# Two 32-row matrix products of a chunk inverse written as full-height products, and the instruction order seeded from a table in the source

## The chip, the cores and the metric

One NeuronCore of a Trainium2 chip runs the whole program in one launch. The time is device microseconds from launch to end, as the median of several executions of the same built program. Beside it stands one profiled execution, whose span runs from its first to its last recorded instruction. The engines have short names in the profile: PE is the matrix engine (PEld its weight loads), DVE the vector engine, ACT the scalar engine, POOL the GpSimd engine and SP the queue that issues the transfers.

## The reference, cut to what matters

The layer is a decoder mixer with two groups of heads, run over 4096 positions of width 1024: one input projection, a gated linear attention group, an RWKV-7 group, one output projection with residual, and two RMS norms. The change touches the RWKV group alone, whose reference is a recurrence over positions:

```python
def _rwkv7_scan(r, decay, k, v, kk, a):
    """S_t = S_{t-1} (diag(w_t) - kk_t^T (a_t * kk_t)) + v_t^T k_t ;  y_t = S_t r_t."""
    def step(S, inp):
        r_t, w_t, k_t, v_t, kk_t, a_t = inp
        sa = jnp.einsum('bhvk,bhk->bhv', S, -kk_t)
        S = (S * w_t[:, :, None, :]
             + sa[..., None] * (kk_t * a_t)[:, :, None, :]
             + v_t[..., None] * k_t[:, :, None, :])
        y = jnp.einsum('bhvk,bhk->bhv', S, r_t)
        return S, y
    _, y = lax.scan(step, S0, xs)
```

Within a chunk of 64 positions the terms `sa` depend on each other through a strictly triangular 64x64 matrix per head, so that a chunk needs the inverse of a unit triangular matrix. The kernel works by chunks and computes that inverse.

## The kernel before

The sequence is cut into 8 blocks of 512 positions. In a block the RWKV heads come as 4 pairs; a pair of heads in one block is a unit, 32 units in all, and a unit has 8 chunks of 64 positions. The two heads of a pair lie in rows 0 to 63 and 64 to 127 of every tile.

Several streams of work are recorded side by side: the weight splitter, the normalisation of x, the projections and preparation of a unit (`rwkv_ab`), the inverse (`rwkv_i`), the chain over the chunks (`rwkv_c`), what follows it (`rwkv_d`), the attention group and the output blocks. The projections are float16 matmuls with 512 moving columns, three for each product, because each operand is split in a high and a low half; the small products of the RWKV unit are float32. A matmul of `both` or `duo` is a pair: the same 128 rows, with weights 64 columns wide in the left and in the right half of the array, which run side by side. That is the shape 128x64 (rows by columns of weights) in the profile, and projections and chain products all have it. Other products use the array in other shapes: 64x128, 64x64, 128x32, 128x128 (transposes) and 32x32.

The inverse of a unit goes in three steps. `rwkv_ab` fills the tile `nb` (`Nb` in the profile) with the triangular matrices from products `DD,bk`, and sends their 32x32 diagonal blocks through memory (`nd`) into a tile `f`. POOL inverts these blocks by a recurrence of 31 steps with two operations each (`tm`, `Tc`), and the result goes through memory again (`td`) back into the diagonal blocks of `nb`. For the last unit alone the recurrence runs on DVE. Then `rwkv_i` makes the block off the diagonal, which is a product of three 32x32 matrices for each head and chunk:

```python
            for q0 in (0, 64):
                V.transpose(Ta[q0:q0 + 32], nb[q0:q0 + 32, :, q0:q0 + 32])
            for c in range(NC):
                for q0 in (0, 64):
                    T.matmul(pl[q0 + 32:q0 + 64, 0, c, :], lhsT=nb[q0:q0 + 32, c, q0 + 32:q0 + 64], rhs=Ta[q0:q0 + 32, c, :],
                             start=True, stop=True)
            V.tensor_copy(Vs, pl[:, 0])
```

and a second set of 16 such products from `Vs` (the same buffer as `Ta`) against `nb`, which ACT copies into `nb`. The first 16 are called the first product below, the second 16 the second product. `rwkv_c` then runs the 8 chunks of the unit one after the other, with three pairs of products per chunk (`ch<-sv,DD`, `ch<-us,Nb`, `ch<-uv,bk`), where ACT or DVE must move each result before the next pair can start.

The order on every engine is made by the program itself while it is built. Each operation is recorded with its predecessors, its engine and an assumed duration. `forward` is a list scheduler over these, with a rank for each operation and two parameters, `keep` (how much a matmul of the shape that PE is in is preferred) and `look` (how far ahead an engine looks). `backward` makes ranks from the other end. `build(guide)` records the streams again so that they follow the start times of an earlier round, which also decides which PSUM bank a stage gets. Before, 11 rounds were run, starting from no guide, and the order whose modelled end was earliest was kept; the instructions were then issued in the order of their modelled start. Every engine works its instructions strictly in that order, and waits where an input is late.

Of the kernel before, what the change touches and what calls it, by code (L numbers as in the profile page):

```python
# [3 lines left out]

# [6 lines left out]
F32 = mybir.dt.float32  # L11
# [3 lines left out]
U8 = mybir.dt.uint8  # L15
# [6 lines left out]
P = 128  # L22
# [3 lines left out]
C = 64  # L26
# [12 lines left out]
SO = 0.3  # L39
# [6 lines left out]
PB = {"ch": 1, "y": 1}  # L46
NBK = 6
NC = TB // C
LOOKS = ((1.0, 0.15),)
PASSES = 5  # L50
PUT_OFF = 1.0
ROUNDS = (LOOKS,) * 11
GUP = 2.0 ** 19
DECAY = math.exp(-0.5)

# [25 lines left out]
CK_GM = 896  # L81
CK_SEL = 1408
NCK = 1536


@with_exitstack
def hymba_kernel(ctx, tc, xT, wt, wg, wo, wua, gup, pk, ck, out):
    nc = tc.nc
    nc.scalar.preload_act_table_set("exp_and_others")
    NT = out.shape[1]  # L90
    NB = NT // TB

    one = ctx.enter_context(tc.tile_pool(name="one", bufs=1))
# [3 lines left out]
    rt = ctx.enter_context(tc.tile_pool(name="rt", bufs=1))  # L97
# [10 lines left out]
    def build(guide):  # L108
# [21 lines left out]
        def parts(ap):  # L130
            if ap.tensor.name == out.tensor.name:
                return []
            if ap.space == DRAM:
                return dram(ap)
            a = ap.start_partition()
            tag = ap.tensor.name.rsplit("_", 1)[0].rstrip("0123456789_")
            if tag in TABLES:
                w = math.prod(ap.tensor.shape[1:])
                return [(ap.tensor.name, i) for i in range(ap.offset % w, ap.offset % w + math.prod(ap.shape[1:]))]
            if tag in FINE:  # L140
                q = FINE[tag]
                return [(ap.tensor.name, h) for h in range(a // q, (a + ap.shape[0] - 1) // q + 1)]
            hs = range(a // 64, (a + ap.shape[0] - 1) // 64 + 1)
            if ap.tensor.name in HEADS:
                o = ap.offset % P // 64
                e = range(2) if ap.ap[-1][1] > 64 else range(o, o + 1)
                return [(ap.tensor.name, h, i) for h in hs for i in e]
            if ap.tensor.name in XS:
                o = ap.offset % (4 * TB) // TB
                e = range(o, o + max(1, math.prod(ap.shape[1:]) // TB)) if ap.dtype == F16 else range(4)  # L150
                return [(ap.tensor.name, h, 2 + i) for h in hs for i in e]
            return [(ap.tensor.name, h) for h in hs]
# [324 lines left out]
        def after(*what):  # L477

            t = 0.0
            for x in what:  # L480
                if isinstance(x, tuple):
                    r = ring.get((x[0], F32))
                    for i in range(x[1] if r else 0):
                        y = r[1][(r[0] + i) % len(r[1])]
                        t = max([t] + [used.get(k, 0.0) for k in parts(y)])
                else:
                    t = max([t] + [ready.get(k, (0.0, ""))[0] for k in parts(x)])
            return t + EL
# [28 lines left out]
        V, S, G, T, D = (Engine(n, e) for n, e in (("V", nc.vector), ("S", nc.scalar), ("G", nc.gpsimd), ("T", nc.tensor), ("D", nc.sync)))  # L517
        lo, hi = slice(0, 64), slice(64, 128)
# [22 lines left out]
        def sb(pool, shape, dt, tag, bufs=1):  # L541

            key = (tag, dt)
            if key not in store:
                store[key] = [pool.tile(shape, dt, tag=f"{tag}_{i}", name=f"{tag}_{i}") for i in range(bufs)]
            if key not in ring:
                ring[key] = [0, store[key]]
            r = ring[key]
            t = r[1][r[0] % len(r[1])]
            r[0] += 1  # L550
            return t
# [5 lines left out]
        f3 = lambda t: t.rearrange("p (c t) -> p c t", c=NC)  # L557
# [26 lines left out]
        for g in range(4):  # L584
            q = slice(32 * g, 32 * g + 32)
# [30 lines left out]
        Gst = [sb(one, [P, P], F32, f"Gst{j}") for j in range(2)]  # L616
        for t in Sst + Gst:
            G.memset(t, 0.0)
        NBUF = 2
        DD = [sb(un, [P, NC, 2, P], F32, f"DD{i}") for i in range(NBUF)]  # L620
        HEADS.update(t.tensor.name for t in DD)
        De, Do = ([t[:, :, :, 64 * e:64 * e + 64] for t in DD] for e in range(2))
        uv1 = sb(un, [P, NC, 2, 64], F32, "uv")
        Nb = [sb(un, [P, NC, 192], F32, f"Nb{i}") for i in range(NBUF)]
        SC = [sb(un, [P, 4, P], F32, f"SC{i}") for i in range(2)]
        for i in range(NBUF):
            G.memset(De[i], 0.0)
# [183 lines left out]
        def rel(st):  # L811
            banks.extend(held.pop(st, []))

        def need(st, n=1):

            rel(st)
            put_off = False
            while True:
                if len(banks) < n:
                    yield lambda: len(banks) >= n  # L820
                banks.sort(key=(lambda t: leave.get(t.tensor.name, 0.0)) if guide else bank_free)
                if len(banks) >= n and (guide or bank_free(banks[n - 1]) <= now[0]):
                    t = leave.get(banks[n - 1].tensor.name, 0.0)
                    if guide and not put_off and t > due(cur[0])[0] + PUT_OFF:
                        put_off = True
                        yield (t,)
                        continue
                    break
                if len(banks) >= n:
                    yield bank_free(banks[n - 1])  # L830
            held[st] = [banks.pop(0) for _ in range(n)]
            return held[st] if n > 1 else held[st][0]
# [98 lines left out]
        def rwkv_ab(u, p, b, xs, LR):  # L931
            de, do, nb = De[u % NBUF], Do[u % NBUF], Nb[u % NBUF]
            cs_ = slice(P * p, P * p + P)
# [131 lines left out]
            for k, q in enumerate((lo, hi)):  # L1065
                for e, o in enumerate((hi, lo)):
                    S.copy(sv[o, k::2, e, :], pv[q, :, e, :])
            units[u] = (DD[u % NBUF], nb, sv, bk, PC, bv, tg)
            done["A"] += 1
# [10 lines left out]

        def rwkv_i(nb):

            Ta = Vs = sb(rt, [P, NC, 32], F32, "Ta", 1)
            yield after(nb)
            for q0 in (0, 64):
                V.transpose(Ta[q0:q0 + 32], nb[q0:q0 + 32, :, q0:q0 + 32])
            yield after(Ta)
            pl = (yield from need("i")).rearrange("p (a c t) -> p a c t", a=2, c=NC)
            for c in range(NC):
                for q0 in (0, 64):  # L1090
                    T.matmul(pl[q0 + 32:q0 + 64, 0, c, :], lhsT=nb[q0:q0 + 32, c, q0 + 32:q0 + 64], rhs=Ta[q0:q0 + 32, c, :],
                             start=True, stop=True)
            V.tensor_copy(Vs, pl[:, 0])
            yield after(Vs)
            for c in range(NC):
                for q0 in (0, 64):
                    T.matmul(pl[q0:q0 + 32, 1, c, :], lhsT=Vs[q0 + 32:q0 + 64, c, :], rhs=nb[q0 + 32:q0 + 64, c, q0 + 32:q0 + 64],
                             start=True, stop=True)
            for q0 in (0, 64):
                S.copy(nb[q0:q0 + 32, :, q0 + 32:q0 + 64], pl[q0:q0 + 32, 1])  # L1100
            rel("i")
# [444 lines left out]
        def stream_i():  # L1546
            for u in range(4 * NB):
                yield lambda: u in invs_
                done["IS"] += 1
                yield from rwkv_i(invs_.pop(u))  # L1550
                done["I"] += 1
# [37 lines left out]
        return steps, forward, backward  # L1589

    with tc.manual_schedule(engines={getattr(mybir.EngineType, e) for e in ("PE", "DVE", "Activation", "Pool", "SP")}):
        guide, best = {}, None
        for looks in ROUNDS:
            steps, forward, backward = build(guide)
            first_order = forward([s.t0 for s in steps])
            mine = first_order
            for keep, look in looks:
                start, end = first_order
                for _ in range(PASSES):
                    start, end = forward(backward(end), keep, look)  # L1600
                    mine = min(mine, (start, end), key=lambda x: max(x[1]))
            if best is None or max(mine[1]) < max(best[2]):
                best = (steps,) + mine
            guide = {s.key: (mine[0][s.n], mine[1][s.n]) for s in steps}
        steps, start, end = best
        for s in sorted(steps, key=lambda s: (start[s.n], s.n)):
            s.f()
# [3 lines left out]
def _layout(d):  # L1611
# [22 lines left out]
    i = np.arange(P)  # L1634
    ck = np.zeros((P, NCK), np.float32)
    ck[:64, CK_BONES] = 1
# [34 lines left out]
```

## Time and profile before

| | |
|---|---|
| median of 3 executions | 2221.82 us (2220.91 to 2226.53) |
| the profiled execution | 2219.66 us |
| its span | 2217.9 us |
| mean granted clock of PE | 0.984 |
| instructions recorded | 75008 |
| data moved by transfers | 326.90 MB, 147 GB/s on average |

The share of busy time says how much of the span an engine had work running. For PE a matmul counts until its last result is written, and the next starts well before that, so that short gaps between starts do not show as idle time. In the rows of a group, the names stand as result<-moving operand,weights, and a float32 product appears as two records, since it passes through the array twice. In a timeline a row is a run of equal instructions on an engine, with its start, its length up to the last end, and in brackets how long the engine was idle before it and what released it.

### The profile page before, as it was taken

The numbers are of one execution on the slowest core, as the hardware profiler recorded it, in microseconds if no ns is written. First come the engines' busy times: TensorE is split into PE (matmuls) and PEld (weight loads), VectorE is DVE, ScalarE is ACT, GpSimd is POOL, SyncE is SP. The second block draws the span as 40 slices with busy tenths as digits, with TensorE's granted clock in tenths as the row PEclk, the third lists the DMA queues.
The fourth block names the chain that finished last, engine by engine and source line by source line (L and its number), as shares of the span: only waits on it lengthen the run. The fifth ranks groups of instructions, "written<-read, shape, count | busy, mean of one in ns | idle before, by whom it ended". The sixth has DMA issues, their size and how long they took to land.

```text
span 2217.9 us, 75008 instructions
## 1 busy us (share of the span) xinstructions
PE 2130.2 (96%) x30680; PEld 1365.4 (62%) x30680; DVE 1705.3 (77%) x3802; ACT 1249.9 (56%) x3229; POOL 877.8 (40%) x2212
## 2 busy tenths in 40 slices
PE   6899999999999999999999999999999999999997
PEld 2556675666755657656675566655666565755664
DVE  8988969588785777768777787858878588684976
ACT  7676675464645456455654556545465464655452
POOL 3462434525253451426425254442533525254400
PEclk8999999999999999999999999999999999999999
DMA  6786655455344643455434554345534465344443
GB/s 202 241 260 179 189 166 165 140 181 165 90 133 141 179 127 101 122 150 179 131 110 120 177 155 129 112 134 163 164 98 124 131 187 159 91 130 126 120 131 96
DMA packets 275454, 326.90 MB, mean 147 GB/s; under 512 B 131572, under 2 KB 132772, under 8 KB 275108
## 3 DMA queue, kind: packets, MB, share of 16 engines
q1 hardware_dynamic: 275108, 322.10, 49.5%
q8 instruction: 240, 3.93, 0.7%
q14 instruction: 106, 0.87, 0.1%
HBM read 276.94 MB, written 45.05 MB: 145 GB/s over the span
## 4 chain that ended last, share of the span: by engine, by line
PE 64%; DVE 19%; DMA 8%; ACT 4%; issue 3%; POOL 2%; SPq 1%; DVEq 0%; ACTq 0%; POOLq 0%
PE bank L532 51%; PE bank L473 8%; PE ch L532 3%; DMA xr<-in_xT_dram 3%; DVE DD L473 2%; DVE nta L473 1%; DVE bk L473 1%; SPq L473 1%; PE y L473 1%; DVE mgr L473 1%; DVE mgg L473 1%; PE y L532 1%; DVE x L473 1%; DMA wdr<-wo 1%; DVE Nb L473 1%
## 5 line engine op out<-in xcount | busy, mean ns | idle before, releaser
L532 PE MATMUL bank<-x,wr 128*64 128x512 f16 x6528 | 799.4, 382 | 8.2 <-ACT x L473 2.7
L473 POOL TENSOR_TENSOR tm<-Tc,f 128x60 f32<-128x60 f32 (+24 forms) x961 | 349.7, 364 | 614.3 <-DMA f<-nd 531.6
L532 PEld LDWEIGHTS <-wr 128*64 128x64 f16 x6528 | 359.8, 111 | 266.6 <-issue 30.7
L473 POOL TENSOR_TENSOR Tc<-Tc,tm 128x60 f32<-128x60 f32 (+24 forms) x961 | 361.2, 376 | 74.1
L532 PE MATMUL bank<-x,wg 128*64 128x512 f16 x3072 | 372.2, 381 | 4.6 <-DVE ki L473 2.0
L532 PE MATMUL bank<-x,wo 128*64 128x512 f16 x2976 | 354.8, 381 | 0.1
L473 POOL TENSOR_TENSOR xacc<-xacc,xr 128x512 f32<-128x512 f32 x98 | 130.3, 1330 | 365.4 <-ACT xr L473 195.8
L532 PEld LDWEIGHTS <-wg 128*64 128x64 f16 x3072 | 174.0, 110 | 123.8 <-issue 7.3
L473 DVE SCALAR_TENSOR_TENSOR sv<-ch,PC,psd 64x64 f32<-64x64 f32 x434 | 122.4, 282 | 145.9 <-PE ch L532 131.8
L532 PEld LDWEIGHTS <-wo 128*64 128x64 f16 x2976 | 161.6, 110 | 116.9 <-issue 4.3
L532 PEld LDWEIGHTS <-x 128*64 128x64 f16 x6240 | 190.1, 110 | 20.9 <-issue 9.4
L532 PE MATMUL bank<-wg,x 128*64 128x128 f16 x6144 | 196.4, 219 | 4.4 <-issue 2.7
L473 ACT ACTIVATE psd<-sv,PC 128x128 f32<-128x128 f32 x248 | 99.1, 399 | 164.6 <-DVE sv L473 142.8
L473 ACT COPY uv<-ch 64x64 f32<-64x64 f32 x496 | 101.7, 205 | 82.1 <-PE ch L532 73.2
L473 ACT COPY us<-ch 64x64 f32<-64x64 f32 x496 | 101.5, 205 | 59.0 <-PE ch L532 50.5
L473 ACT ACTIVATE sa<-bank,mu_s 128x512 f32<-128x512 f32 x104 | 71.4, 687 | 64.7 <-PE bank L532 63.2
L473 DVE COPY_PREDICATED Nb<-mc,bank 64x512 f32<-64x512 uint8 x128 | 92.9, 728 | 6.2 <-PE bank L473 4.4
L473 DVE COPY_PREDICATED DD<-mc,bank 64x512 f32<-64x512 uint8 x128 | 93.5, 731 | 2.7
L532 PEld LDWEIGHTS ch<-sv,DD 128*64 128x64 f32 x992 | 66.1, 138 | 47.0 <-DVE sv L473 15.0
L532 PEld LDWEIGHTS ch<-us,Nb 128*64 128x64 f32 x992 | 66.3, 138 | 45.8 <-ACT us L473 15.4
L532 PEld LDWEIGHTS ch<-uv,bk 128*64 128x64 f32 x992 | 66.1, 138 | 41.5 <-ACT uv L473 12.8
L473 POOL MEMSET Tc<- 32x8 f32 (+1 forms) x160 | 23.5, 147 | 165.5 <-DMA td<-Tc 160.1
(348 smaller groups left out, 3616.9 us busy)
## 6 DMA issues: line engine op xcount, KB each, us to landing
wr<-wdr SPq DMA_DIRECT2D x256, 256.0 KB
wg<-wdr SPq DMA_DIRECT2D x184, 256.0 KB
xr<-in_xT_dram SPq DMA_DIRECT2D x176, 256.0 KB
wo<-wdr SPq DMA_DIRECT2D x128, 256.0 KB
f<-nd SPq DMA_DIRECT2D x128, 128.0 KB
x<-in_wt_dram SPq DMA_DIRECT2D x29, 512.0 KB
wdr<-wo SPq DMA_DIRECT2D x25, 512.0 KB
out_dram<-mgg SPq DMA_DIRECT2D x33, 256.0 KB
```

The source lines that it names most:

```text
L473: put(t0, self.name, d, lag, cols, tiles, tab, outs, ins, lambda: f(*a, **kw))
L532: nc.tensor.matmul(x, lhsT=l, rhs=y, start=start, stop=stop)
```

## The change

Four things differ.

1. A tile `lw` of 9 x 32 columns takes the place of `Ta` and `Vs`, and is the only one of its kind. Before each unit's transposes POOL sets rows 32 to 63 and 96 to 127 of it to zero.
2. The first product becomes, for each chunk, one pair over all 128 rows with weights 64 columns wide (`nb[:, c, 0:P]` in two halves) and 32 moving columns (`lw`). The rows that don't belong to the product meet zeros.
3. DVE's copy of the result becomes a multiplication by a column `lower` that is 1 in rows 32 to 63 and 96 to 127, and 0 elsewhere. The second product becomes a pair with the chunk's 32 columns of `lw` and the 32 beside them as weights, and `nb` as the moving operand.
4. The scheduler starts from a guide that is unpacked from a table in the source (`STARTS`, 24896 start times, one for each recorded operation), runs one round in place of 11, and tries two settings of `keep` and `look`.

```diff
-LOOKS = ((1.0, 0.15),)
+LOOKS = ((0.7, 0.3), (1.0, 0.0))
 PASSES = 5
 PUT_OFF = 1.0
-ROUNDS = (LOOKS,) * 11
+ROUNDS = (LOOKS,) * 1
+COUNTS = ((('d', 0), 19), (('d', 1), 19), (('d', 10), 19), (('d', 11), 19),
...
+STARTS = (
+    "c-qZ92b3Juk=1FsXJ%(M?`l`8w7Xj63=$HO0LcaeCg+UF=*}dAF+qR<b0!@aID!F#v20_T<bX*A4CYKU$p#w}O%g!_AwXewyRNGK@1E|So|zTkv$an%Jsp1kU%BenuV3$)!2g<|2qxs@FH6TRbbte6"
...
+def first_guide():
+
+    d = zlib.decompress(base64.b85decode(STARTS))
+    t, i, g = 0.0, 0, {}
+    for name, n in COUNTS:
+        for k in range(n):
+            t += struct.unpack_from("<h", d, 2 * i)[0] / 10
+            g[(name, k)] = (t, t + 0.3)
+            i += 1
+    return g
...
+        lw = sb(one, [P, NC + 1, 32], F32, "lw")
+        G.memset(lw, 0.0)
+        lower = sb(one, [P, 1], F32, "lower")
+        G.memset(lower, 0.0)
+        for q0 in (32, 96):
+            G.memset(lower[q0:q0 + 32], 1.0)
...
-            Ta = Vs = sb(rt, [P, NC, 32], F32, "Ta", 1)
+            Ta = Vs = lw
             yield after(nb)
+            for q0 in (32, 96):
+                G.memset(Ta[q0:q0 + 32, 0:NC], 0.0)
             for q0 in (0, 64):
-                V.transpose(Ta[q0:q0 + 32], nb[q0:q0 + 32, :, q0:q0 + 32])
+                V.transpose(Ta[q0:q0 + 32, 0:NC], nb[q0:q0 + 32, :, q0:q0 + 32])
             yield after(Ta)
             pl = (yield from need("i")).rearrange("p (a c t) -> p a c t", a=2, c=NC)
             for c in range(NC):
-                for q0 in (0, 64):
-                    T.matmul(pl[q0 + 32:q0 + 64, 0, c, :], lhsT=nb[q0:q0 + 32, c, q0 + 32:q0 + 64], rhs=Ta[q0:q0 + 32, c, :],
-                             start=True, stop=True)
-            V.tensor_copy(Vs, pl[:, 0])
+                both(pl[:, 0, c, :], nb[:, c, 0:P], Ta[:, c, :], True, True)
+            V.tensor_scalar_mul(Vs[:, 0:NC], pl[:, 0], lower)
             yield after(Vs)
             for c in range(NC):
-                for q0 in (0, 64):
-                    T.matmul(pl[q0:q0 + 32, 1, c, :], lhsT=Vs[q0 + 32:q0 + 64, c, :], rhs=nb[q0 + 32:q0 + 64, c, q0 + 32:q0 + 64],
-                             start=True, stop=True)
+                duo(pl[:, 1, c, :], [pl[h, 1, c, :] for h in (lo, hi)], [Vs[:, c:c + 2, :].rearrange("p c t -> p (c t)")] * 2,
+                    [nb[:, c, 32:64], nb[:, c, 96:128]], True, True)
...
-        guide, best = {}, None
+        guide, best = first_guide(), None
```

The order of nearly every instruction on every engine moves. Three places matter for what follows. The first is PE's order around the first product of one unit, before: the 32x32 products stand between other float32 products of other shapes (`gtwo` and `bones` are columns of ones for sums, `ident` is the identity for transposes).

```order
L473 MATMUL bank_0_189<-ki_238,gtwo_101 32x128 x4
L473 MATMUL bank_0_187<-r_200,bones_105 32x128 x4
L473 MATMUL bank_0_186<-Ta_252,Nb_0_137 32x32 x16
L473 MATMUL bank_0_190<-ident_76,bk_243 128x128 x4
L473 MATMUL bank_0_188<-ident_76,bk_243 128x128 x4
L473 MATMUL bank_0_189<-ident_76,v_201 128x128 x4
L473 MATMUL bank_0_186<-Nb_0_137,Ta_252 32x32 x16
```

The same unit in the changed kernel:

```order
L685 MATMUL bank_0_190<-x_1_2_0_89,wr_217 64x512
L685 MATMUL bank_0_187<-lw_134,Nb_0_139 64x32 x2
L685 MATMUL bank_0_190<-x_1_3_0_90,wr_217 64x512
L685 MATMUL bank_0_187<-lw_134,Nb_0_139 64x32 x6
L685 MATMUL bank_0_187<-lw_134,Nb_0_139 64x32 x8
L626 MATMUL bank_0_191<-r_202,bones_105 32x128 x4
L626 MATMUL bank_0_192<-gbc_229,gtwo_101 32x128 x4
L626 MATMUL bank_0_188<-ident_76,bk_241 128x128 x4
L626 MATMUL bank_0_192<-ki_251,gtwo_101 32x128 x4
L685 MATMUL bank_0_187<-Nb_0_139,lw_134 64x32 x16
```

The 16 products of a set now stand among the projections (`x` against `wr`), whose shape in the array they share, and the other float32 products stay together.

The second place is POOL's queue at the start of a unit's recurrence, before, where it begins as soon as its memsets are done and `f` has landed:

```order
L473 TENSOR_TENSOR Tc_248<-Tc_248,tm_249 128x8
L473 MEMSET Tc_248 128x256
L473 MEMSET Tc_248 32x8 x4
L473 TENSOR_TENSOR tm_249<-Tc_248,f_0_216 128x31
L473 TENSOR_TENSOR Tc_248<-Tc_248,tm_249 128x31
```

and in the changed kernel:

```order
L626 TENSOR_TENSOR Tc_247<-Tc_247,tm_248 128x8
L626 MEMSET Tc_247 128x256
L626 MEMSET Tc_247 32x8 x4
L626 MEMSET lw_134 32x256 x2
L626 TENSOR_TENSOR tm_248<-Tc_247,f_0_218 128x31
L626 TENSOR_TENSOR Tc_247<-Tc_247,tm_248 128x31
```

The two memsets of `lw` stand ahead of the recurrence, in 28 of the 32 units before its first step and in the others within its first three. They may not run before the second product of the unit before has read `lw` on PE.

The third place is PE's order in the chain over the chunks, at a spot where the products `DD,bk` of the next unit start. Before, seven pairs of the chain follow each other with a single other product between them:

```order
L532 MATMUL ch_267<-us_268,Nb_0_138 64x64 x2
L473 MATMUL bank_0_187<-DD_0_134,bk_242 128x128
L532 MATMUL ch_267<-uv_136,bk_243 64x64 x2
L532 MATMUL ch_267<-sv_256,DD_0_135 64x64 x2
L532 MATMUL ch_267<-us_268,Nb_0_138 64x64 x2
L532 MATMUL ch_267<-uv_136,bk_243 64x64 x2
L532 MATMUL ch_267<-sv_256,DD_0_135 64x64 x2
L532 MATMUL ch_267<-us_268,Nb_0_138 64x64 x2
L473 MATMUL bank_0_190<-DD_0_134,bk_242 128x128
```

In the changed kernel, at the same products of the same unit:

```order
L626 MATMUL bank_0_188<-DD_0_136,bk_240 128x128
L626 MATMUL bank_0_187<-DD_0_136,bk_240 128x128
L685 MATMUL ch_268<-uv_138,bk_241 64x64 x2
L685 LDWEIGHTS wg_244
L685 MATMUL bank_0_189<-x_1_0_0_87,wg_244 64x512
```

All 16 `DD,bk` products stand ahead of the chain's pair, and a projection (`x` against `wg`) fills the places between this pair and the next.

More of the change, by code (lines that the diff above doesn't have):

```diff
@@ L1 @@
+import base64
 import heapq
 import math
+import struct
+import zlib
 from contextlib import ExitStack
@@ L48 @@
 NC = TB // C
-LOOKS = ((1.0, 0.15),)
+LOOKS = ((0.7, 0.3), (1.0, 0.0))
 PASSES = 5
 PUT_OFF = 1.0
-ROUNDS = (LOOKS,) * 11
+ROUNDS = (LOOKS,) * 1
+COUNTS = ((('d', 0), 19), (('d', 1), 19), (('d', 10), 19), (('d', 11), 19), (('d', 12), 19), (('d', 13), 19), (('d', 14), 19), (('d', 15), 19), (('d', 16), 19), (('d', 17), 19), (('d', 18), 19), (('d', 19), 19), (('d', 2), 19), (('d', 20), 19), (('d', 21), 19), (('d', 22), 19), (('d', 23), 19), (('d', 24), 19), (('d', 25), 19), (('d', 26), 19), (('d', 27), 19), (('d', 28), 19), (('d', 29), 19), (('d', 3), 19), (('d', 30), 19), (('d', 31), 21), (('d', 4), 19), (('d', 5), 19), (('d', 6), 19), (('d', 7), 19), (('d', 8), 19), (('d', 9), 19), ('a', 9745), ('c', 3379), ('e', 109), ('g', 1720), ('i', 736), ('init', 42), ('o', 2464), ('p', 4920), ('w', 603), ('x', 568))
```

135 lines of the change are left out of this document (added).

## The prediction

> **What bounds the kernel now.** I read the page's busy times first, then the busy time by stretches, then the groups by form, the timeline around an inverse, and last the waits.
>
> ```profile
> PE 2130.2 (96%) x30680; PEld 1365.4 (62%) x30680; DVE 1705.3 (77%) x3802; ACT 1249.9 (56%) x3229; POOL 877.8 (40%) x2212
> PE 64%; DVE 19%; DMA 8%; ACT 4%; issue 3%; POOL 2%; SPq 1%; DVEq 0%; ACTq 0%; POOLq 0%
> ...
> 0.00:50.00 50.00, 31.03 (x272) 13.26 (x274) 41.84 (x139) 36.07 (x62) 16.73 (x38) 0.83 0.62 193
> 50.00:100.00 50.00, 47.52 (x638) 28.91 (x636) 46.44 (x117) 37.00 (x68) 15.71 (x20) 1.00 0.73 233
> 100.00:150.00 50.00, 43.51 (x592) 29.50 (x588) 43.64 (x120) 31.33 (x61) 30.22 (x68) 0.90 0.81 260
> 150.00:200.00 50.00, 44.53 (x612) 28.50 (x610) 45.83 (x120) 37.31 (x91) 21.24 (x52) 0.93 0.65 199
> 2150.00:2218.00 68.00, 53.08 (x718) 32.15 (x714) 43.12 (x103) 22.43 (x68) 0.00 (x0) 0.93 0.34 106
> ```
>
> PE is busy for 96% of the span and makes up 64% of the chain that ended last. It is idle for 2217.9 - 2130.2 = 87.7 us: 33.4 us in the first 200 us, where the weights are still being split, 14.9 us in the last 68 us, and 39.4 us in the 1950 us between (columns after the length: PE, PEld, DVE, ACT, POOL). So in the long middle the time is PE's own work, and an edit there is worth what it adds to or takes from that work, plus what it does to 39 us of waits.
>
> **The change part by part.** *The products that go.* The groups by form give their cost, and the timeline shows where it comes from:
>
> ```profile
> L473 PE MATMUL bank<-Ta,Nb 32*32 32x32 f32 x1024 | 23.3, 194 | 3.2 <-DVE nva L473 2.8 <-DVE Ta L473 0.3
> L473 PE MATMUL bank<-Nb,Ta 32*32 32x32 f32 x1024 | 22.7, 194 | 0.5 <-DVE Ta L473 0.3
> ...
> 538.48 0.61 PE L473 MATMUL bank<-x,wgs 128*32 128x512 f16 x8
> 539.02 0.69 PE L473 MATMUL bank<-Ta,Nb 32*32 32x32 f32 x32
> 539.65 0.62 PE L532 MATMUL bank<-x,wr 128*64 128x512 f16 x4
> ```
>
> 64 sets of 16 products take 23.3 + 22.7 = 46.0 us, or 0.72 us a set. In the timeline the set holds PE from 539.02 to 539.65, 0.63 us, and it starts late: the two groups of four before it have a pitch of about 0.216 us, so that the next start would have been due at 538.48 + 0.43 = 538.91. The missing 0.11 us is the price of turning the array into another shape. A set's 32 records, two at a time, have a pitch of (0.69 - 0.191) / 15 = 0.033 us, with 0.191 us the length of one record (fence below).
>
> *The products that come.* 16 float32 products of shape 128x64 with 32 moving columns do not occur before. The nearest rows are the same shape with 64 moving columns, and the records' shortest, median and longest durations in a stretch at full clock:
>
> ```profile
> 888.35 1.10 PE L532 MATMUL y<-DD,sv 128*64 128x64 f32 x32
> ...
> L473 PE MATMUL bank<-Ta,Nb x128: 191/191/212, 848.6 to 1071.4; 32*32 32x32 f32 x128
> L532 PE MATMUL ch<-us,Nb x128: 218/222/271, 832.1 to 1093.9; 128*64 128x64 f32 x128
> L473 PE MATMUL bank<-DD,bk x128: 272/272/373, 858.3 to 1050.8; 64*128 64x128 f32 x128
> ```
>
> From above: 32 records, two at a time, in 1.10 us, a pitch of (1.10 - 0.222) / 15 = 0.0585 us. If this pitch is set by the 64 moving columns, half as many columns go at about the 0.033 us of the 32x32 set, the bound from below. If it is set by loading the weights, it stays, since the new products have the same 64 weight columns. The durations speak for the weights. The longest record of a form is the one whose weights were not loaded ahead, and its excess over the median is 212 - 191 = 21 ns with 32 columns of weights, 271 - 222 = 49 ns with 64, and 373 - 272 = 101 ns with 128. It goes with the columns, and 49 ns of load for each pass leave no room for a pitch of 33. I take 0.0585: 15 x 0.0585 + 0.033 for the last pass, behind which a projection can follow, is 0.91 us a set, and 64 x 0.91 - 46.0 = **+12.3 us**. From below it is 64 x 16 x 0.033 - 46.0 = -12.2 us.
>
> The Trainium skill says, in "TensorE: Matmul & The Clock Gate", section "LDWEIGHTS (loading the stationary operand)", that a load takes the number of weight columns divided by 1.2 in ns, whatever the number of rows, which is 53 ns for 64 columns. By that rule a set costs 16 x 53 = 0.85 us and the term is +8.5 us, an estimate from that page; the rule speaks against this change, and the three excesses in the trace agree with it.
>
> *The turns of the array.* With 32x32 gone, so are its turns, which the 0.72 us already hold. Counted over the whole of PE's order, the other changes of shape go from 531 to 553: 22 x 0.1 = **+2.2 us**.
>
> *POOL's memsets.* The two in front of each recurrence (the second place of the order) wait for the second product of the unit before, and the whole recurrence is queued behind them. Unit 7, counted from 0, shows what that means:
>
> ```profile
> L473 POOL MEMSET Tc<- 128x256 f32 x32 | 10.1, 316 | 160.1 <-DMA td<-Tc 160.1
> ...
> 538.81 0.37 POOL L473 TENSOR_TENSOR tm<-Tc,f 128x31 f32<-128x31 f32 x1 [8.67 <-DMA f<-nd]
> 565.74 0.22 POOL L473 TENSOR_TENSOR Tc<-Tc,tm 128x8 f32<-128x8 f32 x1
> ...
> 546.28 0.69 PE L473 MATMUL bank<-Nb,Ta 32*32 32x32 f32 x32
> 576.32 0.69 PE L473 MATMUL bank<-Ta,Nb 32*32 32x32 f32 x32
> ```
>
> The recurrence began when `f` landed, 8 us before unit 6's second product ended at 546.97. That is no longer allowed. The loop is now two memsets at 0.316 us, the recurrence of 565.96 - 538.81 = 27.15 us, and 576.32 - 565.96 = 10.36 us through memory, the transposes and the queues: 38.1 us from a second product to the next unit's first. In the new order I count PE's work between these two (each matmul at its pitch) for the 15 odd units up to 29: 37 to 57 us, and 37 to 42 in ten of them. So the order has made room for the loop, with almost none to spare: 1.2 us short in sum at 38.1, but 18 us if the loop takes 3 us longer. Both are bounds; I take **+3 us**. The memsets' own 64 x 0.316 = 20 us lie on an engine with 60% to spare.
>
> *DVE.* The scaled copy replaces
>
> ```profile
> L473 DVE COPY Ta<-bank 128x256 f32<-128x256 f32 x32 | 13.4, 418 | 3.9 <-PE bank L473 3.5
> L473 DVE TENSOR_SCALAR nva<-bank 128x128 f32<-128x128 f32 x95 | 27.3, 287 | 33.9 <-PE bank L473 30.6 <-ACT bk L473 2.0
> ```
>
> The lower bound is the copy's 418 ns, the upper two of the half-sized scaled ones, 574 ns. At most 32 x 0.16 = 5 us on an engine that is 77% busy, between two sets that the order keeps 1 us or more apart by other PE work, counted in 31 of the 32 units. I take 0; uncovered it would cost those 5 us.
>
> *The order.* The part of the waits that a better order can reach is the chain over the chunks:
>
> ```profile
> PE ch L532 <- ACT us L473: 7.8, 11, 1.7
> PE ch L532 <- DVE sv L473: 7.2, 9, 1.8
> PE ch L532 <- ACT uv L473: 3.8, 7, 0.8
> ...
> 1524.63 1.03 PE L532 MATMUL bank<-x,wr 128*64 128x512 f16 x8
> 1525.70 0.49 PE L473 MATMUL bank<-DD,bk 64*128 64x128 f32 x2
> 1526.81 0.34 PE L532 MATMUL ch<-uv,bk 128*64 128x64 f32 x4 [0.62 <-ACT uv L473]
> 1528.03 0.34 PE L532 MATMUL ch<-sv,DD 128*64 128x64 f32 x4 [0.88 <-DVE sv L473]
> 1528.92 0.34 PE L532 MATMUL ch<-us,Nb 128*64 128x64 f32 x4 [0.56 <-ACT us L473]
> 1529.78 0.48 PE L532 MATMUL ch<-uv,bk 128*64 128x64 f32 x4 [0.52 <-ACT uv L473]
> 1532.06 0.48 PE L532 MATMUL ch<-sv,DD 128*64 128x64 f32 x4 [1.79 <-DVE sv L473]
> ```
>
> It costs 7.8 + 7.2 + 3.8 = 18.8 us, and this is the third place of the order: links of the chain that follow each other with nothing between take 0.9 to 2.3 us from start to start, where a link itself is 0.12 us of PE's time. I counted in both orders how much PE work lies between successive links (a projection pair at (1.03 - 0.38) / 3 = 0.217 us). Of 743 links, 29 had less than 1.0 us before and 15 have now, and what they lack in sum goes from 15.7 to 7.5 us: **-8 us**. The bounds are 0, if the waits turn up elsewhere, and -16, if the order is as much better at the 20 us of other waits in the middle, for which I found no count that differs. The tail is alike: from the last unit's second product to the end there are 54 us of PE work before and 55 now, and in the first 200 us the splitting of the weights sets the pace in both.
>
> *The sum.* 12.3 + 2.2 + 3 - 8 = +9.5 us. The profiled execution took 2219.66 us, its span and 1.8 us around it, so it goes to 2229.2; it was 2.2 us under the median, so the median goes from 2221.8 to **2231 us**, 0.4% slower.
>
> **The rivals.** *The order gives back all that the products cost.* For it: a table of start times can hold the outcome of a much longer search than 11 rounds. Against it: outside the chain the counts are alike. With the full -16 the sum is +1.5, 2223 us.
>
> *The products run at the pace of their moving columns.* This is the other side: if the loads of the two column halves run further ahead than one pass, the pitch is 0.033 and not 0.0585. The point from which it decides is a pitch of about 0.047 us, where 64 sets cost the same as before. For it: in no row does a weight load take visibly longer than the pass that it hides behind, because in every float32 form of the trace both have the same number of columns. Against it: the three excesses. The sum is -12.2 + 2.2 + 3 - 8 = -15, **2207 us**.
>
> The same page of the Trainium skill gives, in "Back-to-back issue gap", a gap of N / 2.4 + 2.5 ns for N moving columns with a floor of about 25 ns, and no weight load in it; by that rule this rival would be the forecast, and no row here has fewer moving than weight columns to test it.
>
> *The loop through POOL decides.* If the loop takes 41 and not 38 us, PE stops at the first product of the odd units, with every projection queued behind it: 12.3 + 2.2 + 18 - 8 = +24.5, 2246 us. For it: the recurrence is the slow part and shares work with a busy DVE. Against it: PE, being slower than planned by the products, arrives later too.
>
> That the change does not do what it says is out: no 32x32 product is left in the order.
>
> **How the numbers follow.** The forecast has a chance of 0.54, with its own range of 2223 to 2240; the order giving back everything 0.24; the moving columns' pace 0.12; the loop 0.10. The range of 2209 to 2247 leaves out the lower half of the second rival and the tails of the last. About 0.3%, 6.7 us, is what a measurement of this kernel tells from no change: faster by more is the second rival and the tail of the first, 0.16; within it lie most of the first and the low end of the forecast, 0.27; slower is the rest, 0.57.
>
> **What would show it.** Right: the groups `bank<-lw,Nb` and `bank<-Nb,lw` together at 55 to 60 us busy (46.0 before), a run of x32 of them in 1.05 to 1.15 us, chain waits near 10 us, PE idle below 85 us. Wrong: a run of x32 in about 0.75 us (the moving columns' pace); PE waiting for DVE `lw` or POOL by more than 10 us in sum (the loop); chain waits at 18 us again, or PE idle under 70 us (the order did less or more than its counts).

## The result, and the profile after

The changed kernel took 2228.48 us (median of 20 runs, 2223.38 to 2234.31) where the kernel before took 2220.93 us in 20 runs timed beside them. The ratio is 1.0029 with a 95% interval of 1.0019 to 1.0038: **6.4 us slower**, between 4.2 and 8.4. (The plain medians differ by 7.6 us; the text goes by the ratio, because the interval belongs to it.) That is half of what the two products alone were priced at; the experiments take the rest apart.

The execution that was profiled is the slowest of the 20, 2234.31 us with a span of 2232.5. So rows of one place are used below to size one operation, and medians to say what an edit is worth.

First the busy times, the chain that ended last and the stretches of the changed kernel (columns after the length: PE, PEld, DVE, ACT, POOL, then PE's granted clock, the share of the DMA engines and GB/s), to set beside those of before:

```profile
PE 2138.1 (96%) x30680; PEld 1394.2 (62%) x30680; DVE 1708.8 (77%) x3802; ACT 1252.7 (56%) x3229; POOL 903.6 (40%) x2280
PE 61%; DVE 15%; DMA 7%; POOL 3%; issue 3%; ACT 2%; SPq 2%; DVEq 0%; POOLq 0%; ACTq 0%
...
0.00:50.00 50.00, 32.87 (x282) 15.07 (x284) 41.39 (x135) 35.12 (x61) 16.72 (x43) 0.83 0.63 192
50.00:100.00 50.00, 45.08 (x716) 29.34 (x714) 42.08 (x109) 34.19 (x61) 14.78 (x16) 1.00 0.71 216
100.00:150.00 50.00, 38.29 (x376) 23.49 (x372) 41.41 (x99) 28.38 (x53) 25.51 (x59) 0.83 0.77 244
150.00:200.00 50.00, 45.91 (x657) 30.70 (x655) 44.97 (x129) 41.06 (x99) 25.65 (x69) 0.97 0.76 239
2165.00:2232.00 67.00, 53.49 (x711) 33.09 (x705) 42.55 (x100) 21.28 (x63) 0.00 (x0) 0.92 0.35 108
```

PE is idle for 2232.5 - 2138.1 = 94.4 us, 6.7 more than before. 37.9 us of it lie in the first 200 us (33.4 before), and the largest fall is in one row: PE is busy for 38.29 us between 100 and 150, where it was busy for 43.51. There PE waited 6.4 us at one place for a weight that ACT had to split; what that costs in the median run is not known. In the long middle PE is idle for 43.1 us (39.4 before).

The products in the groups by form, in the timeline, and the range of their durations (shortest, median, longest in ns):

```profile
L685 PE MATMUL bank<-lw,Nb 128*64 128x32 f32 x1024 | 37.4, 222 | 5.4 <-DMA Nb<-td 2.5 <-DVE lw L626 2.3 <-issue 0.2
L685 PE MATMUL bank<-Nb,lw 128*64 128x32 f32 x1024 | 35.7, 221 | 1.2 <-DVE lw L626 1.1
...
661.36 3.00 PE L685 MATMUL bank<-x,wo 128*64 128x512 f16 x26
664.19 1.07 PE L685 MATMUL bank<-lw,Nb 128*64 128x32 f32 x32
665.09 1.25 PE L685 MATMUL bank<-x,wo 128*64 128x512 f16 x10
666.17 1.07 PE L685 MATMUL bank<-Nb,lw 128*64 128x32 f32 x32
667.08 1.68 PE L685 MATMUL bank<-x,wo 128*64 128x512 f16 x14
668.59 0.60 PE L685 MATMUL bank<-x,wr 128*64 128x512 f16 x4
...
L685 PEld LDWEIGHTS bank<-lw,Nb x128: 132/138/140, 855.8 to 1083.1; 128*64 128x64 f32 x128
L685 PE MATMUL bank<-lw,Nb x128: 192/223/243, 855.8 to 1083.1; 128*64 128x32 f32 x128
```

A run of 32 records takes 1.07 us, so the pitch of a slot of two records is (1.07 - 0.223) / 15 = 0.0565 us. The busy time of the two groups is 37.4 + 35.7 = 73.1 us, 1.14 us a set, yet the next projection starts 0.90 us after the set. The difference is the tail of the last record, which runs beside the projection. A group's busy time is therefore not what a set takes from PE; the time from start to start is.

PE's waits that the prediction named, and POOL's longest (us in total, times, longest):

```profile
PE ch L685 <- DVE sv L626: 4.4, 7, 1.5
PE ch L685 <- ACT uv L626: 3.9, 5, 1.6
PE bank L685 <- DVE lw L626: 3.4, 6, 1.0
PE ch L685 <- ACT us L626: 0.7, 1, 0.7
...
POOL tm L626 <- DMA f<-nd: 319.7, 24, 31.6
POOL lw L626 <- PE bank L685: 206.6, 25, 24.9
```

The chain waits are 4.4 + 3.9 + 0.7 = 9.0 us (18.8 before). POOL's memsets stand still for 206.6 us until the second product of the unit before is through, but PE waits for `lw` for 3.4 us only.

### The profile page after: what moved, and what is told of

Read it like the earlier page. It is cut to its first block, busy times and chain, and to the rows that moved or that the text cites. A ratio compares the mean times of both kernels' runs of the same rounds, so it can differ in the third digit from the quotient of the medians.

```text
span 2232.5 us, 75143 instructions
## 1 busy us (share of the span) xinstructions
PE 2138.1 (96%) x30680; PEld 1394.2 (62%) x30680; DVE 1708.8 (77%) x3802; ACT 1252.7 (56%) x3229; POOL 903.6 (40%) x2280
## 4 chain that ended last, share of the span: by engine, by line
PE 61%; DVE 15%; DMA 7%; POOL 3%; issue 3%; ACT 2%; SPq 2%; DVEq 0%; POOLq 0%; ACTq 0%
PE bank L685 49%; PE bank L626 6%; PE ch L685 3%; DVE DD L626 2%; SPq L626 2%; POOL tm L626 2%; POOL Tc L626 2%; PE y L626 1%; DVE nta L626 1%; PE y L685 1%; DVE Nb L626 1%; DMA xr<-in_xT_dram 1%; DMA rn<-bcda 1%; DVE mgg L626 1%; DVE bk L626 1%
## 5 line engine op out<-in xcount | busy, mean ns | idle before, releaser
L626 POOL TENSOR_TENSOR tm<-Tc,f 128x60 f32<-128x60 f32 (+24 forms) x961 | 355.5, 370 | 393.2 <-DMA f<-nd 319.7
L626 POOL MEMSET lw<- 32x256 f32 (+1 forms) x65 | 19.8, 305 | 241.4 <-PE bank L685 206.6
```

Of the source, the lines that this page charges most:

```text
L626: put(t0, self.name, d, lag, cols, tiles, tab, outs, ins, lambda: f(*a, **kw))
```

## The experiments

Each ratio is against the kernel before, timed in the same session; 0.001 is 2.2 us. Where two edited kernels are compared, it is by the difference of their ratios, which is known to 3 or 4 us at best. "Order" is the sequence of instructions on every engine. The code lines give an edit in short: what a step issued, and what it issues now at the same place; `...` marks what is left out.

**1. The old products in the new order.** The steps of the new products emit the old ones:

```
-both(pl[:, 0, c, :], nb[:, c, 0:P], Ta[:, c, :], True, True)
+for q0 in (0, 64):
+    nc.tensor.matmul(pl[q0 + 32:q0 + 64, 0, c, :], lhsT=nb[q0:q0 + 32, c, q0 + 32:q0 + 64], rhs=Ta[q0:q0 + 32, c, :], ...)
...
```

> The changed kernel with its order, memsets and scaled copies untouched; only the inverse's products are the old ones again (32x32 weights, 32 moving columns), each pair at the place of the pair that it replaces. Theory (the loads of 64 weight columns set the pace of the new products): a set goes from 0.93 us to 0.74 us from start to start, 64 x 0.19 = 12 us, less 0.7 us for six more places where the array turns: about 11 us under the changed kernel, so 2215 to 2219 us, and some 5 us under the kernel before, because the order keeps its gain. Rival 1 (the products cost nothing, the new order or the loop through POOL cost the time): it stays at 2228 us. Rival 2 (the order gave nothing back): 2221 us or more.

Measured: 2214.84 us, ratio 0.9980 (0.9965 to 0.9994), 10.9 us under the changed kernel. The timeline at the place shown above:

```profile
652.12 3.00 PE L685 MATMUL bank<-x,wo 128*64 128x512 f16 x26
655.04 0.69 PE L1243 MATMUL bank<-lw,Nb 32*32 32x32 f32 x32
655.67 1.27 PE L685 MATMUL bank<-x,wo 128*64 128x512 f16 x10
656.87 0.69 PE L1249 MATMUL bank<-Nb,lw 32*32 32x32 f32 x32
657.49 1.70 PE L685 MATMUL bank<-x,wo 128*64 128x512 f16 x14
659.02 0.60 PE L685 MATMUL bank<-x,wr 128*64 128x512 f16 x4
```

From the first projection to the row of `wr`, with the same work between, it is 659.02 - 652.12 = 6.90 us here and 668.59 - 661.36 = 7.23 us in the changed kernel. Two sets make the difference, so one costs 0.165 us more, and 64 sets 10.6 us, in line with the 10.9 us of the medians. The products cost time, and the order gave some of it back: both rivals fall.

**2. The new products in the old order.** The other way round, on the kernel before:

```
-V.transpose(Ta[q0:q0 + 32], nb[q0:q0 + 32, :, q0:q0 + 32])
+nc.vector.transpose(lwide[q0:q0 + 64, 0:NC], nb[q0:q0 + 64, :, q0:q0 + 32])
-V.tensor_copy(Vs, pl[:, 0])
+nc.vector.tensor_scalar_mul(lwide[:, 0:NC], pl[:, 0], lower)
...
+nc.tensor.matmul(pl[h, 0, c, :], lhsT=nb[:, c, h], rhs=lwide[:, c, :], ...)
+nc.tensor.matmul(pl[h, 1, c, :], lhsT=lwide[:, c:c + 2, :].rearrange("p c t -> p (c t)"), rhs=nb[:, c, q0 + 32:q0 + 64], ...)
```

> The kernel before with its order on all engines untouched; only the inverse's products are the new ones (all rows, 64 weight columns, 32 moving columns), and the copy is the scaled one. No memsets: the transposes take 64 rows each, so that the zero block beside each 32x32 block brings the zeros. Theory: 64 x 0.19 = +12 us of products and no gain from the order, so 2231 to 2236 us, 10 to 15 us over the kernel before; a run of x32 takes 1.07 us. Rival 1 (the products cost nothing): 2221 us. Rival 2 (part of the products lies in waits of PE that the old order has anyway): 2224 to 2229 us.

Measured: 2236.49 us, ratio 1.0076 (1.0060 to 1.0092), 16.9 us slower, a little more than expected. A run of x32 takes 1.07 us here too. Without the new order the change would have cost well over twice what it did.

**3. Twice the moving columns.** The changed kernel, with products that move 64 columns:

```
-both(pl[:, 0, c, :], nb[:, c, 0:P], Ta[:, c, :], True, True)
+for h in (lo, hi):
+    nc.tensor.matmul(o[h, 32 * c:32 * c + 64], lhsT=nb[:, c, h], rhs=Ta[:, c:c + 2, :].rearrange("p c t -> p (c t)"), ...)
...
```

> The changed kernel; its new products move 64 columns in place of 32 (the second half is the next chunk's and is overwritten by the next product). Order and everything else as in the changed kernel. Theory (weight loads set the pace): a run of x32 stays at 1.07 to 1.12 us, and the time within 2 us of the changed kernel, 2227 to 2231 us. Rival (the moving columns set the pace): the pitch goes from 0.0565 to about 0.1 us, x32 runs of 1.7 us, 64 x 0.65 = +40 us, 2265 us or more.

Measured: 2226.81 us, ratio 1.0040 (1.0027 to 1.0053), 2.4 us over the changed kernel's ratio, with intervals that overlap.

```profile
659.11 3.00 PE L685 MATMUL bank<-x,wo 128*64 128x512 f16 x26
661.94 1.10 PE L1244 MATMUL bank<-lw,Nb 128*64 128x64 f32 x32
662.87 1.25 PE L685 MATMUL bank<-x,wo 128*64 128x512 f16 x10
663.95 1.07 PE L1244 MATMUL bank<-Nb,lw 128*64 128x64 f32 x32
...
666.37 0.60 PE L685 MATMUL bank<-x,wr 128*64 128x512 f16 x4
...
L1244 PE MATMUL bank<-lw,Nb x128: 219/222/270, 852.9 to 1080.8; 128*64 128x64 f32 x128
```

The stretch is 666.37 - 659.11 = 7.26 us against 7.23. The pitch of the first set goes from 0.0565 to (1.10 - 0.222) / 15 = 0.0585 us, and the second set's run stays at 1.07 us: 32 more moving columns cost 2 ns a slot at most. The moving columns don't set the pace.

**4. Half the weight columns.** The changed kernel, still over all 128 rows, but loading only the 32 columns whose result is used:

```
-both(pl[:, 0, c, :], nb[:, c, 0:P], Ta[:, c, :], True, True)
+for q0 in (0, 64):
+    nc.tensor.matmul(pl[q0 + 32:q0 + 64, 0, c, :], lhsT=nb[:, c, q0 + 32:q0 + 64], rhs=Ta[:, c, :], ...)
...
+    nc.tensor.matmul(pl[q0:q0 + 32, 1, c, :], lhsT=Vs[:, c, :], rhs=nb[:, c, q0 + 32:q0 + 64], ...)
```

> The changed kernel, order and everything else untouched; its products still go over all 128 rows, but load only the 32 weight columns whose result is used. Theory (the number of weight columns sets the pace): the pitch falls from 0.0565 to about 0.033 us, a run of x32 from 1.07 to about 0.70 us, 64 x 0.36 = 23 us less, or 16 us less if each set now pays 0.11 us for turning the array into 32-column pieces: 2205 to 2213 us. Rival (the 128 rows, or the float32 passes themselves, set the pace): the run stays at 1.07 us and the time at 2228 us.

Measured: 2215.64 us, ratio 0.9984 (0.9971 to 0.9997), 10.0 us under the changed kernel. The timeline and the durations:

```profile
655.96 3.00 PE L685 MATMUL bank<-x,wo 128*64 128x512 f16 x26
658.89 0.70 PE L1243 MATMUL bank<-lw,Nb 128*32 128x32 f32 x32
659.52 1.27 PE L685 MATMUL bank<-x,wo 128*64 128x512 f16 x10
...
662.88 0.60 PE L685 MATMUL bank<-x,wr 128*64 128x512 f16 x4
...
L1243 PEld LDWEIGHTS bank<-lw,Nb x128: 106/113/113, 850.3 to 1076.8; 128*32 128x32 f32 x128
L1243 PE MATMUL bank<-lw,Nb x128: 189/196/217, 850.3 to 1076.8; 128*32 128x32 f32 x128
```

The pitch is (0.70 - 0.196) / 15 = 0.0336 us, that of the 32x32 products, with four times their rows. So in these products neither the rows nor the moving columns set the pace, but the weight columns: 0.0565 us with 64 and 0.0336 with 32, 23 ns for 32 columns. Half the weight columns are also half the rows of the result, which this edit can't tell apart; the load's own records, 138 ns against 113, speak for the load. The stretch to the row of `wr` is as long as in the first experiment, 662.88 - 655.96 = 6.92 us. The expected 16 to 23 us were too much, because they took the price of turning the array once or not at all. It is paid on both sides: the set starts 658.89 - 655.96 = 2.93 us after the 26 projections began (2.83 in the changed kernel), and of the 0.63 us from its start to the next projection its 16 slots are only 16 x 0.0336 = 0.54. In the changed kernel 16 x 0.0565 = 0.90 us, all of the set's time: 64-column pieces between 64-column projections pay no turn.

**5. No memsets.** The changed kernel; the block beside each 32x32 block is zero in `nb`, so a transpose of 64 rows brings the zeros along:

```
-for q0 in (32, 96):
-    G.memset(Ta[q0:q0 + 32, 0:NC], 0.0)
-V.transpose(Ta[q0:q0 + 32, 0:NC], nb[q0:q0 + 32, :, q0:q0 + 32])
+nc.vector.transpose(Ta[q0:q0 + 64, 0:NC], nb[q0:q0 + 64, :, q0:q0 + 32])
```

> The changed kernel, order untouched, without POOL's 64 memsets: the two transposes of each unit take 64 rows in place of 32 and bring the zeros from the zero block beside each 32x32 block. So the recurrence no longer waits for the unit before. Theory (the loop through POOL costs about the +3 us that the prediction gave it, or less): 0 to 4 us under the changed kernel, 2221 to 2228 us where the kernel before takes 2219 to 2221. Rival (the loop decides): 10 to 18 us under it, 2207 to 2215 us.

Measured: 2222.72 us, ratio 1.0011 (1.0002 to 1.0020), 4.0 us under the changed kernel. The larger transpose is free (437 ns on average, 431 with 32 rows). POOL's longest wait in this kernel:

```profile
POOL tm L626 <- DMA f<-nd: 513.5, 27, 41.5
```

This is where the 206.6 us of the memsets' wait went: 319.7 + 206.6 = 526.3 us before the edit, 513.5 us after it, now all of it for `f`, the input of the recurrence. Most units' recurrence would not have begun earlier anyway. The rival, in which the loop decides, falls. Where the 4.0 us lie is not shown: PE's waits for `lw` are 2.8 + 0.9 = 3.7 us here and were 3.4 with the memsets.

**6. The memsets six times.** The opposite edit on the changed kernel:

```
-    G.memset(Ta[q0:q0 + 32, 0:NC], 0.0)
+    [nc.gpsimd.memset(Ta[q0:q0 + 32, 0:NC], 0.0) for _ in range(6)]
```

> The changed kernel, order untouched, with each of POOL's memsets issued six times in a row: 10 more of 0.305 us, which lengthens the loop from second product to memsets, recurrence and next first product by 3.05 us in every unit. By the prediction's count of PE work beside the loop this costs 18 us (2242 to 2247 us) if the loop is 38 us as it said. Rival 1 (the recurrence of a unit has more room than that count gave it): within 2 us of the changed kernel, 2225 to 2230 us. Rival 2 (every unit waits for the loop already): 32 x 3 = 98 us more.

Measured: 2233.76 us, ratio 1.0058 (1.0043 to 1.0073), 6.4 us over the changed kernel: neither the 18 us of the prediction's bound nor nothing.

```profile
POOL tm L626 <- DMA f<-nd: 266.6, 21, 26.8
...
PE bank L685 <- DVE lw L626: 7.0, 9, 2.7
```

POOL still waits for `f` 21 times, where it was 24 in the changed kernel and 27 without memsets. So in a few more units the memsets now end later than `f` lands, and PE's waits for `lw` go from 3.4 to 7.0 us. That is about half of the loss; where the rest lies is not shown.

**7. Half the weight columns and no memsets.** Experiments 4 and 5 together, which differs from the changed kernel by

```
-for q0 in (32, 96):
-    G.memset(Ta[q0:q0 + 32, 0:NC], 0.0)
-V.transpose(Ta[q0:q0 + 32, 0:NC], nb[q0:q0 + 32, :, q0:q0 + 32])
+nc.vector.transpose(Ta[q0:q0 + 64, 0:NC], nb[q0:q0 + 64, :, q0:q0 + 32])
...
-both(pl[:, 0, c, :], nb[:, c, 0:P], Ta[:, c, :], True, True)
+for q0 in (0, 64):
+    nc.tensor.matmul(pl[q0 + 32:q0 + 64, 0, c, :], lhsT=nb[:, c, q0 + 32:q0 + 64], rhs=Ta[:, c, :], ...)
...
```

> The two edits together on the changed kernel's order: only the 32 weight columns whose result is used, and transposes over 64 rows in place of the memsets. Theory: the product part as in the run with 32 weight columns alone (0.998 of the kernel before), less what the run without memsets gains: 2210 to 2216 us. Rival (faster products turn the loop into the limit, so that the memsets matter more here): 2200 to 2208 us.

Measured: 2213.89 us, ratio 0.9975 (0.9962 to 0.9989), 5.6 us under the kernel before and faster than both kernels. The memsets' part is 2.0 us here, from two ratios whose intervals overlap, and not more than with the slower products: nothing says that faster products make the loop the limit.

**8. The old products, planned anew.** The changed kernel with `rwkv_i` of the kernel before, so that the plan, which starts from the new table, is made with the old steps' costs:

```
-Ta = Vs = lw
+Ta = Vs = sb(rt, [P, NC, 32], F32, "Ta", 1)
...
+T.matmul(pl[q0 + 32:q0 + 64, 0, c, :], lhsT=nb[q0:q0 + 32, c, q0 + 32:q0 + 64], rhs=Ta[q0:q0 + 32, c, :], start=True, stop=True)
+V.tensor_copy(Vs, pl[:, 0])
...
```

> The changed kernel's table of start times as the start of the search, but with the old products (32x32), no memsets and the plain copy, and the order planned anew from these. Theory (the order is worth about what the run with the old products in the new order showed, 0.998 of the kernel before, and planning the right costs loses nothing): 2210 to 2217 us. Rival (the table fits only the steps that it was searched for, and a new plan from it loses its gain): 2219 us or more.

Measured: 2219.92 us, ratio 1.0005 (0.9988 to 1.0021). No gain is left that this run can tell from nothing, though the plan was made with the steps that are issued. The reading that fits is that the table's worth lies in the very order that it was searched for, and that a plan made from it for other steps is another order; which moves lost the gain is not shown.

**9. The order alone.** The changed kernel's order, with 32x32 products as in experiment 1, the plain copy and no memsets:

```
-G.memset(Ta[q0:q0 + 32, 0:NC], 0.0)
-V.tensor_scalar_mul(Vs[:, 0:NC], pl[:, 0], lower)
+nc.vector.tensor_copy(Vs[:, 0:NC], pl[:, 0])
...
```

> The changed kernel's order on all engines with the work of the kernel before: 32x32 products at the places of the new ones, no memsets, the plain copy. What is left of the change is its order. Theory (the order gives 8 us, as the prediction counted for the chain; the memsets cost 4, as the run without them showed): 8 us under the kernel before, a ratio of 0.996, 2210 to 2213 us where that takes 2219 to 2221. Rival (the gain of the run without memsets came from the new products that they serve, and the order is worth 4 us, as with the old products and the memsets): a ratio of 0.998.

Measured: 2212.74 us, ratio 0.9976 (0.9963 to 0.9990), 5.3 us under the kernel before. This is the order's own worth; the interval, 2.2 to 8.2 us, does not tell the theory's 8 from the rival's 4. The chain waits of this kernel:

```profile
PE ch L685 <- ACT uv L626: 3.3, 5, 1.6
PE ch L685 <- DVE sv L626: 3.2, 5, 0.8
...
PE ch L685 <- ACT us L626: 1.3, 4, 0.7
```

They are 7.8 us, 11 under the kernel before. The others follow the order as well, whatever the products: 10.7 us in experiment 1 and 8.0 in experiment 4, but 20.3 us in experiment 2, in the old order.

**10. Half the weight columns in the old order.** Experiment 2 with the products of experiment 4:

```
-nc.tensor.matmul(pl[h, 0, c, :], lhsT=nb[:, c, h], rhs=lwide[:, c, :], ...)
+nc.tensor.matmul(pl[q0 + 32:q0 + 64, 0, c, :], lhsT=nb[:, c, q0 + 32:q0 + 64], rhs=lwide[:, c, :], ...)
...
```

> The order of the kernel before, with products over all 128 rows but only the 32 weight columns that are used, transposes over 64 rows and the scaled copy: it differs from the run of the new products in the old order (1.0076) by the number of weight columns alone. Theory (the weight columns are the whole cost there too, 5 us of it by waits that longer sets cause in the old order): within 3 us of the kernel before, a ratio of 0.999 to 1.0015. Rival (4 to 5 of those 17 us come from the scaled copy and the larger transposes on DVE): a ratio of 1.002 to 1.003.

Measured: 2221.09 us against 2216.77, ratio 1.0017 (1.0002 to 1.0033), between theory and rival, with an interval that holds both. Taken as it stands, some 3.8 us (0.4 to 7.3) of experiment 2 are not the weight columns'. The waits and the DVE group name a part:

```profile
PE bank L1103 <- DVE lwide L1095: 3.6, 3, 2.2
PE bank L1112 <- DVE lwide L1105: 1.1, 4, 0.4
...
L1105 DVE TENSOR_SCALAR lwide<-bank,lower 128x256 f32<-128x256 f32 x32 | 15.3, 478 | 4.5 <-PE bank L1103 4.1
```

PE waits 4.7 us for `lwide`, where it waited 0.6 us for `Ta` before; the copy takes 478 ns in place of 418. The weight columns' share in the old order is 1.0076 - 1.0017 = 0.0059, 13.1 us.

## Why the prediction was right, and which term was off

The prediction was 2231 us, 9.5 us slower than the kernel before. The change went that way, by 6.4 us. Term by term:

| term | predicted | measured |
|---|---|---|
| products | +12.3 | +10.6 by the stretch of two sets; +10.9 (experiment 1), +10.0 (4), +8.0 (5 against 7) by ratios; +13.1 in the old order (2 against 10) |
| order, with the turns elsewhere | -8 + 2.2 = -5.8 | -5.3 (experiment 9) |
| POOL's memsets | +3 | +4.0 (experiment 5), +2.0 (4 against 7), +0.9 (1 against 9, with DVE's scaled copy in it) |
| DVE's scaled copy | 0 | not measured alone |
| sum | +9.5 | +6.4 (4.2 to 8.4) |

**The products: right in mechanism, a little too large.** "I take 0.0585" was 2 ns too much, since with 32 moving columns the pitch is 0.0565. "0.033 for the last pass" was 23 ns too little, since a whole slot of 0.0565 us passes before the next projection starts. The two nearly cancel: a set takes 0.90 us from start to start, where 0.91 was foretold. What is left of the difference lies in the set that goes: it costs 0.90 - 0.165 = 0.735 us with its turns, where its busy time gave 0.72. So 64 sets cost 10.6 us more and not 12.3. Doubling the moving columns did nothing that can be measured, and halving the weight columns took everything back, so the rival of the moving columns' pace is out.

The reading that led to 0.0585 was weaker than it looked. In its three rows the moving columns are as many as the weight columns, so the excesses of 21, 49 and 101 ns could have come from either. The prediction says that this is so in every float32 form, and there it is wrong; rows of the kernel before in the same stretch:

```profile
L473 PE MATMUL bank<-ki,gtwo x16: 272/273/297, 876.9 to 1070.5; 128*32 128x128 f32 x16
L473 PE MATMUL bank<-ident,bk x32: 272/273/329, 873.1 to 1072.4; 128*128 128x128 f32 x32
```

With 32 weight columns and 128 moving ones the excess is 297 - 273 = 24 ns at most, which speaks for the weights and could have been read beforehand. But with 128 weight columns over 128 rows it is 329 - 273 = 56 ns and not 101. And the changed kernel's own products, with 64 weight columns, have their longest record only 243 - 223 = 20 ns above the median, though 243 - 192 = 51 above the shortest. So the excess over the median does not measure a load in every form. The choice of 0.0585 came out right, and in part by luck; it is experiments 3 and 4 that show the cause.

The Trainium skill's rule in "TensorE: Matmul & The Clock Gate", section "LDWEIGHTS (loading the stationary operand)", agrees with these runs in its slope: the weight columns divided by 1.2 give 27 ns for 32 more columns, an estimate from that page, and 23 were measured over 128 rows. It agrees with the pitch of 32 weight columns in the independence from rows, 0.033 us with 32 rows and 0.0336 with 128. The load records of 128 weight columns don't bear that out: their median is 188 ns over 64 rows (`DD,bk`, before) and 141 over 128 rows (`ident,bk`, before). The formula in its section "Back-to-back issue gap" counts moving columns alone, and the section says itself that this is too little for few of them; here it gives about 25 ns, an estimate from that page, for the slot that took 56.5.

**The order: right in its sum.** The count of chain links with too little work between them foretold 8 us, less 2.2 for the turns elsewhere. The chain waits fell by 9.8 us in the changed kernel and by 11 in experiment 9, and all of the order together is worth 5.3 (2.2 to 8.2). The rival in which the order gives back everything is out. Neither of the two parts was measured alone. The prediction also took the first 200 us to be alike: PE is idle there for 33.9 to 39.6 us in the eight executions in the new order that were profiled, and for 33.4 to 34.8 in the three in the old one. So some of the gain may be lost there; how much is not shown.

**The memsets: right in size, wrong in their edge.** The bound of "18 us if the loop takes 3 us longer" failed: experiment 6 made it 3.05 us longer and lost 6.4. The count took it that the recurrence begins when the memsets end. POOL's waits show that in most units it begins when `f` lands, and there a wait ahead of the later one costs nothing. That the +3 came out near the 0.9 to 4.0 of the runs is luck in part: it was a choice between two bounds of that count.

**What was misread.** The mark "the groups together at 55 to 60 us busy" came out at 73.1 although the sets take what was foretold, 0.90 us from start to start. The old groups' 0.72 us a set came close to what a set costs only because two things that have nothing to do with each other, the last record's tail inside the group's time and the turn outside it, are about equal. The other marks held: a run of x32 at 1.07 us, chain waits near 10. PE's idle time came out at 94.4 and not below 85 us, in an execution 5.8 us over the median.

What stays open: the terms that were measured in the new order, -5.3 + 10.6 and 1 to 4 us for the memsets, make 6 to 9 us, and each ratio is known to 2 or 3 us. A single microsecond can't be placed.

## What to carry to other kernels

Before making a small product larger for the sake of a simpler shape, count its weight columns: in a row of small products they were the price here, while rows of zeros and more moving columns were nearly free. Price a set by the time from start to start between neighbours in the timeline, never by its group's busy time. When an edit adds a wait to an engine, look first at what that engine waits for next; if that comes later anyway, the new wait only changes its name.

## What the runs showed of the hardware that was not expected

Products with the array's full height are as fast as those with a quarter of it: a pitch of 0.0336 us with 128 rows and 0.033 with 32, at 32 weight columns. Turning the array goes with the columns of a piece too: sets of 32 columns pay the same 0.1 us on either side with 128 rows as with 32, and sets of 64 columns between projections of 64 pay nothing that shows. And a DVE transpose of 64 rows takes 437 ns where one of 32 rows takes 431, which is what made the memsets superfluous.
